# Attention in a two-layer encoder: product with v on token rows, softmax division behind it, four transposes back to channels

## The chip, the core and the metric

The kernel runs on one core of a Trainium2 chip. The metric is the device time in microseconds (us) of one execution. Three runs of the kernel before gave 1927.76, 1929.54 and 1931.59 us, with a median of 1929.54 us. One further execution was profiled; its own time was 1926.47 us, of which 1924.7 us are the span of the profile. The TensorE clock has two levels here, 2.4 and 1.2 GHz; the profile shows the granted clock as 1.00 and 0.50.

## What is computed

Two layers over 512 tokens and 1024 channels; each is a half-step SwiGLU, a mixer, and a second half-step SwiGLU. The mixer has windowed attention with 8 heads on 2 key heads, beside a state-space branch; both are normalized and go through one output projection. Cut to what matters:

```python
s = jnp.where(mask, q @ k * 0.125 + bias, NEG_INF)      # 128 queries, up to 384 keys
m = jnp.maximum(jnp.max(s, axis=-1, keepdims=True), sink)
p = jnp.exp(s - m)
denom = jnp.sum(p, axis=-1, keepdims=True) + jnp.exp(sink - m)
o = jnp.einsum('bnkgqs,bnskd->bnqkgd', p / denom, v)     # a: (512, 512)
x = x + concat(rms_norm(a, attn_out_norm), rms_norm(ssm, ssm_out_norm)) @ w_out
```

All of it is float32. Large products are made of three single-pass products of rounded parts (`mm3`, lines 216 to 218); attention's product with v and the transposes are plain float32.

## The kernel before

All activations lie with channels on the 128 partitions and 512 tokens along the row. Weights stream from memory in blocks of up to 128x2048; ScalarE rounds each block to its high part (line 199) and VectorE, in some places GpSimd, makes the low part (line 202), in two halves. There are two buffers for the high parts and two for the low parts, so a block's rounding waits until the products with the block two before it are done.

The mixer's work is a list of named steps, `ORDER` (line 43): a program walks through it and emits each step. The framework then places the instructions of each engine by an estimate of its own, so that steps of the list interleave; the order that came out is fixed in the program. Each engine runs its own list strictly in order.

The steps that matter here run per block n of 128 tokens and key head kv, so there are eight units per layer; a block has 2, 3, 3 and 2 key blocks kb:

- `as` (`a_scores`, line 951): for each of 4 heads two products into one PSUM bank (965, 966); VectorE adds the bias and finds the maximum (968); ScalarE makes the exponentials and their sums (975).
- `an` (`a_norm`, line 979): VectorE forms the denominators (985, 986) and divides the exponentials, one instruction per head (990).
- `ao` (`a_out`, line 992): for each key block, TensorE transposes the four heads' probabilities (998); the copy out of PSUM is VectorE's for odd key blocks (1001) and ScalarE's for even ones (1003).
- `pv` (`a_pv`, line 1008): the product with v (1013). v is the stationary operand, 64 columns of it per key head, the turned probabilities of four heads are the moving one, 512 wide; the two key heads use the two halves of the array. The result has channels on partitions. VectorE multiplies by the norm's gain (1022), ScalarE rounds to the high part (1024) and squares (1025), VectorE makes the low part (1027), GpSimd (VectorE for the last block) adds squares up into `acc_a` (1029, 1030).
- `ws` (`norm_ws`): the output projection's state-space half, products of 12 matmuls for each of eight output blocks, each followed by a multiplication and an addition to x (1066, 1068).
- After the list come the `wa` products, the output projection's attention half. They need all four blocks of the attention output, the high parts first and the low parts soon after. The sum of squares is turned into a factor by `rstd_a`, which begins with four matmuls against a column of ones (325), and `rstd_b` (341, 344).
- `ffn` follows; its first products need the high and low parts of the new x. VectorE makes the low parts (283), one 128x512 block at a time. In layer 0 VectorE also has the many small preparations of layer 1's state-space tables to do.

Of the kernel before, what the change touches and what calls it, by code (L numbers as in the profile page):

```python
# [9 lines left out]
F32R = mybir.dt.float32r  # L10
I32 = mybir.dt.int32
AF = mybir.ActivationFunctionType
# [4 lines left out]
P = 128  # L17
T = 512
# [24 lines left out]
l0 ui0 pu2 pu3 ui2 ui1 si0 k l1 ui3 v vt q0 si1 sc0 sc1 l2 q1 si2 l3 L0 q2 si3 q3 sc2 L1 so0 L2 as0 sc3 L3 an0  # L43
so2 as1 so1 so3 yt0 ao0 yt1 an1 as2 an2 ao1 glu as3 ao2 sn pv0 as4 ws0 an3 ao3 ws1 as5 an4 ws2 ao4 ws3 an5 as6
an6 pv1 ws4 ws5 ao5 as7 ws6 an7 ao7 ao6 pv2 ws7 pv3
# [30 lines left out]
class Emit:  # L76
# [242 lines left out]
    def rstd_a(self, acc, n, w=T):  # L319

        V = self.V
        b = self.bank()
        c = w // P
        for j in range(c):
            self.T.matmul(b[:, j:j + 1], acc[:, j * P:(j + 1) * P], self.ones, start=True, stop=True)  # L325
        s = self.slot()
        m, y, t = s[:, 0:c], s[:, 4:4 + c], s[:, 8:8 + c]
        V.tensor_scalar(m, b[:, 0:c], 1.0 / n, EPS, op0=ALU.mult, op1=ALU.add)
        self.bfree(b)
# [425 lines left out]
    def mixer(self, l, st, after):  # L755
# [223 lines left out]
        def a_norm(n, kv):  # L979
            k0, k1 = at[n]["k"]  # L980
            nk = (k1 - k0) * P
            sm = at[n]["sm"]
            c4 = slice(kv * 4, kv * 4 + 4)
            den, t = sm[:, 16:24], sm[:, 24:32]
            V.tensor_tensor(out=den[:, c4], in0=den[:, c4], in1=t[:, c4], op=A)
            V.reciprocal(den[:, c4], den[:, c4])
            for i in range(4):
                hd = kv * 4 + i
                p = at[n]["p"][kv][:, i * T:i * T + nk]
# [18 lines left out]
        def a_pv(n):  # L1008
            k0, k1 = at[n]["k"]
            o = self.bank()  # L1010
            for kb in range(k0, k1):
                for kv in range(2):
                    TE.matmul(o[kv * 64:kv * 64 + 64], vt[:, kb * P + kv * 64:kb * P + kv * 64 + 64], at[n][kv][kb - k0],
                              start=kb == k0, stop=kb == k1 - 1, tile_position=(0, kv * 64))
            for kv in range(2):
                self.free(*at[n][kv])

            if not abuf:
                abuf.extend([self.slot(4, True), self.slot(4, True)])
            cs = slice(n * T, (n + 1) * T)  # L1020
            f, q = self.slot(), self.slot()
            V.tensor_tensor(out=f.rearrange("p (i t) -> p i t", i=4), in0=o.rearrange("p (i t) -> p i t", i=4),
                            in1=ga.rearrange("p (i o) -> p i o", o=1).to_broadcast([P, 4, P]), op=M)
            S.copy(abuf[0][:, cs].bitcast(F32R), f)
            S.activation(q, o, AF.Square)
            self.bfree(o)
            V.tensor_tensor(out=abuf[1][:, cs].bitcast(F32R), in0=f, in1=abuf[0][:, cs], op=B)
            eng = V if n == 3 else Gp
            eng.tensor_tensor(out=q[:, 0:256], in0=q[:, 0:256], in1=q[:, 256:512], op=A)
            eng.tensor_tensor(out=acc_a[:, n * P:(n + 1) * P], in0=q[:, 0:P], in1=q[:, P:2 * P], op=A)  # L1030
            self.free(f, q, at[n]["sm"])
# [91 lines left out]
        def norm_ws(d):  # L1123
            if d == 0:
# [6 lines left out]
                 "as": lambda i: a_scores(*units[i]), "an": lambda i: a_norm(*units[i]),  # L1131
                 "ao": lambda i: a_out(*units[i]), "pv": a_pv, "yt": y_turn, "glu": lambda _: glu(),
# [13 lines left out]
        dg = self.rstd_a(acc_a, 512)  # L1146
# [125 lines left out]
def _cols(v):  # L1272
    return v.reshape(-1, P).T
# [11 lines left out]
def lay(inp):  # L1285
# [3 lines left out]
    g = []  # L1289
# [70 lines left out]
```

## Time and profile before

| | |
|---|---|
| median of three runs | 1929.54 us (1927.76 to 1931.59) |
| profiled execution, its own time | 1926.47 us |
| its span | 1924.7 us |
| TensorE busy | 1865.4 us, 97% |
| VectorE busy | 1123.4 us, 58% |
| ScalarE busy | 626.5 us, 33% |
| GpSimd busy | 714.8 us, 37% |

The stretches that the change touches are about 485 to 608 us (layer 0: attention, then `wa`, then the start of the second SwiGLU) and 1430 to 1560 us (layer 1). In the rows, PE is TensorE's matmul stream, PEld its loading of stationary operands, DVE VectorE, ACT ScalarE, POOL GpSimd. A float32 matmul appears as two matmul records (two passes), a transpose as one. The duration of one matmul runs until its result has drained, and successive ones overlap; how fast a train of them goes is seen from the start times.

### The profile page before, as it was taken

The page shows a single profiled execution, that of the slowest core. Times are in us where ns is not written, and L with a number is a line of the kernel's source. Part 1 is how long each engine was busy: PE and PEld are TensorE (multiplying, and loading weights), DVE is VectorE, ACT ScalarE, POOL GpSimd, SP SyncE. Part 2 cuts the span into 40 slices and gives each one's busy share as a digit, 9 for nine tenths or more (in the row PEclk, how much of TensorE's full clock was granted, in tenths as well). Part 3 has the DMA queues.
Part 4 walks back from the last instruction along what each step waited for, and adds up shares of the span by engine and source line. Part 5 has one row for each costly group of instructions (what it writes and reads, how often), then busy time and mean ns, then how long its engine had stood idle before and what let it go on. Part 6 is the DMA issues. An engine that isn't in the chain of part 4 may idle for free. (4 is left out here: it accounts for less than half of the span.)

```text
span 1924.7 us, 23787 instructions
## 1 busy us (share of the span) xinstructions
PE 1865.4 (97%) x9416; PEld 1510.5 (78%) x9416; DVE 1123.4 (58%) x1713; ACT 626.5 (33%) x954; POOL 714.8 (37%) x596
## 2 busy tenths in 40 slices
PE   8999999997998999999999999999989999999997
PEld 6888888886767888888878888888766678888886
DVE  8646545569888635355674453436697673434435
ACT  5223223322733323223332222224236342222223
POOL 2049899237233015093483351103452230201102
PEclk9999999998899999999999999999989999999998
DMA  5533434576011223233333234424640122222321
GB/s 202 165 121 123 160 125 156 160 244 229 31 67 61 98 104 121 99 131 115 108 134 114 99 133 129 137 98 142 232 171 23 65 79 98 88 107 82 107 97 46
DMA packets 86232, 231.12 MB, mean 120 GB/s; under 512 B 31160, under 2 KB 38504, under 8 KB 70376
## 3 DMA queue, kind: packets, MB, share of 16 engines
q1 hardware_dynamic: 84888, 228.51, 35.0%
q8 instruction: 74, 1.21, 0.3%
q10 hardware_dynamic: 1232, 1.09, 0.2%
q14 instruction: 38, 0.31, 0.0%
HBM read 201.11 MB, written 34.75 MB: 123 GB/s over the span
## 5 line engine op out<-in xcount | busy, mean ns | idle before, releaser
L216 PE MATMUL psum<-blk,whi 128*128 128x512 f32 (+1 forms) x2446 | 954.4, 393 | 9.7 <-ACT blk L277 6.4
L217 PE MATMUL psum<-blk,whi 128*128 128x512 f32 (+1 forms) x2446 | 953.7, 390 | 8.2 <-DVE blk L283 8.2
L218 PE MATMUL psum<-blk,wlo 128*128 128x512 f32 (+1 forms) x2446 | 952.0, 390 | 1.4 <-DVE wlo L202 0.9
L216 PEld LDWEIGHTS psum<-blk,whi 128*128 128x128 f32 x2446 | 462.0, 189 | 108.6 <-ACT blk L277 6.9
L217 PEld LDWEIGHTS psum<-blk,whi 128*128 128x128 f32 x2446 | 461.2, 189 | 106.3 <-DVE blk L283 12.9
L218 PEld LDWEIGHTS psum<-blk,wlo 128*128 128x128 f32 x2446 | 461.2, 189 | 97.9 <-DVE wlo L202 2.0
L199 ACT CAST whi<-raw 128x1024 fp32r<-128x1024 f32 (+1 forms) x310 | 303.4, 1027 | 683.3 <-PE psum L217 476.1
L202 DVE TENSOR_TENSOR wlo<-raw,whi 128x1024 fp32r<-128x1024 f32 (+1 forms) x288 | 419.2, 1490 | 40.6 <-ACT whi L199 30.7
L381 DVE TENSOR_TENSOR blk<-psum,blk 128x512 f32<-128x512 f32 x88 | 60.6, 691 | 343.7 <-PE psum L218 340.2
L407 POOL TENSOR_TENSOR xtile<-xtile,blk 128x512 f32<-128x512 f32 x64 | 88.1, 1378 | 374.3 <-DVE blk L405 370.1
L405 DVE SCALAR_TENSOR_TENSOR blk<-psum,blk 128x512 f32<-128x512 f32 x94 | 64.9, 690 | 214.9 <-PE psum L218 208.9
L380 ACT ACTIVATE blk<-blk 128x512 f32<-128x512 f32 x88 | 55.4, 632 | 301.9 <-DVE blk L378 297.4
L694 POOL TENSOR_TENSOR blk<-blk,blk 128x512 f32<-128x512 f32 x64 | 86.8, 1367 | 92.5 <-PE psum L707 51.7
L378 DVE TENSOR_TENSOR blk<-psum,blk 128x512 f32<-128x512 f32 x88 | 60.2, 688 | 85.7 <-PE psum L218 85.2
L295 POOL TENSOR_TENSOR blk<-blk,blk 128x512 f32<-128x512 f32 x30 | 45.6, 1518 | 155.1 <-ACT blk L288 154.3
L202 POOL TENSOR_TENSOR wlo<-raw,whi 128x1024 fp32r<-128x1024 f32 x22 | 60.4, 2752 | 110.2 <-ACT whi L199 110.0
L695 POOL TENSOR_TENSOR blk<-blk,blk 128x512 f32<-128x512 f32 x64 | 88.1, 1378 | 29.3 <-PE psum L707 14.4
L697 POOL TENSOR_TENSOR blk<-blk,blk 128x512 f32<-128x512 f32 x49 | 77.7, 1590 | 2.4
L385 DVE TENSOR_TENSOR blk<-blk,blk 128x512 fp32r<-128x512 f32 x88 | 76.4, 870 | 0.7 <-ACT blk L384 0.7
L283 DVE SCALAR_TENSOR_TENSOR blk<-xtile,consts,blk 128x512 fp32r<-128x512 f32 x48 | 58.7, 1239 | 10.6 <-ACT blk L277 10.6
L1068 POOL TENSOR_TENSOR xtile<-xtile,blk 128x512 f32<-128x512 f32 x24 | 33.7, 1425 | 72.8 <-DVE blk L1066 68.1
L295 POOL TENSOR_TENSOR blk<-blk 128x512 f32<-128x512 f32 x12 | 19.1, 1595 | 99.4 <-ACT blk L288 99.2
(227 smaller groups left out, 1343.0 us busy)
## 6 DMA issues: line engine op xcount, KB each, us to landing
raw<-w SPq DMA_DIRECT2D x123, 1024.0 KB, 4.8
raw<-w SPq DMA_DIRECT2D x32, 896.0 KB, 4.5
fd<-blk SPq DMA_DIRECT2D x32, 256.0 KB, 2.7
ed<-blk SPq DMA_DIRECT2D x32, 256.0 KB, 3.4
blk<-ed SPq DMA_DIRECT2D x32, 256.0 KB, 5.9
blk<-fd SPq DMA_DIRECT2D x32, 256.0 KB, 4.3
tb<-blk SPq DMA_DIRECT2D x12, 512.0 KB, 2.9
blk<-tb SPq DMA_DIRECT2D x24, 256.0 KB, 6.3
```

Source lines behind the costliest of these rows:

```text
L199: self.S.copy(hi[:, c], raw[:, c])
L202: eng.tensor_tensor(out=lo[:, c], in0=raw[:, c], in1=hi[:, c].bitcast(F32), op=ALU.subtract)
L216: t.matmul(out, wh, xh, start=start, stop=False)
L217: t.matmul(out, wh, xl, start=False, stop=False)
L218: t.matmul(out, wl, xh, start=False, stop=stop)
L295: eng.tensor_tensor(out=acc, in0=acc, in1=sq, op=ALU.add)
L385: V.tensor_tensor(out=lo.bitcast(F32R), in0=s, in1=hi, op=ALU.subtract)
L405: V.scalar_tensor_tensor(t, ps, 0.5, R, op0=ALU.mult, op1=ALU.mult)
L407: (V if last else self.G).tensor_tensor(out=self.x[d], in0=self.x[d], in1=t, op=ALU.add)
L694: Gp.tensor_tensor(out=full(o), in0=mat(a), in1=pwo(w, 0), op=M)
L695: Gp.tensor_tensor(out=full(t), in0=mat(b), in1=pwo(w, 1), op=M)
L697: Gp.tensor_tensor(out=o, in0=o, in1=t, op=sg)
```

## The change

The product with v is turned round. The turned probabilities of one head and key block (128 keys by 128 queries) become the stationary operand and 64 columns of v the moving one, so that the result has tokens on partitions and the eight heads' 64 channels side by side. The division by the denominator is no longer applied to the exponentials; it is applied once per block to that result, in one VectorE instruction that reads PSUM (line 1013 of the new file). ScalarE squares the result with a running sum per token (1016), which gives the sum of squares without the ones-matmuls and without GpSimd. Four transposes per block (1026) then bring channels back to partitions; gain, high part and low part follow as before (1029, 1032, 1033). All copies of turned probabilities are ScalarE's (991). The channels of the attention output now stand in their natural order, and the weights and gains are laid out to match. In `ORDER` the `an` steps are gone, `pt` steps are new, and `ws7` stands behind `pv3` instead of before it.

```diff
-so2 as1 so1 so3 yt0 ao0 yt1 an1 as2 an2 ao1 glu as3 ao2 sn pv0 as4 ws0 an3 ao3 ws1 as5 an4 ws2 ao4 ws3 an5 as6
-an6 pv1 ws4 ws5 ao5 as7 ws6 an7 ao7 ao6 pv2 ws7 pv3
+so2 as1 so1 so3 yt0 ao0 yt1 as2 ao1 glu as3 ao2 sn pv0 as4 ws0 pt0 ao3 ws1 as5 ws2 ao4 ws3 as6
+pv1 ws4 pt1 ws5 ao5 as7 ws6 ao7 ao6 pv2 pv3 pt2 ws7 pt3
...
-        def a_norm(n, kv):
...
-                V.tensor_scalar(p, p, den[:, hd:hd + 1], None, op0=M)
...
-                if kb % 2:
-                    V.tensor_copy(pt, b)
-                else:
-                    S.copy(pt, b)
+                S.copy(pt, b)
...
-            for kb in range(k0, k1):
-                for kv in range(2):
-                    TE.matmul(o[kv * 64:kv * 64 + 64], vt[:, kb * P + kv * 64:kb * P + kv * 64 + 64], at[n][kv][kb - k0],
-                              start=kb == k0, stop=kb == k1 - 1, tile_position=(0, kv * 64))
+            for kv in range(2):
+                for i in range(4):
+                    c = (kv * 4 + i) * 64
+                    for kb in range(k0, k1):
+                        TE.matmul(o[:, c:c + 64], at[n][kv][kb - k0][:, i * P:(i + 1) * P],
+                                  vt[:, kb * P + kv * 64:kb * P + kv * 64 + 64], start=kb == k0, stop=kb == k1 - 1)
...
+            V.tensor_tensor(out=den, in0=den, in1=t, op=A)
+            V.reciprocal(den, den)
+            f, q = self.slot(), self.slot()
+            V.tensor_tensor(out=f.rearrange("p (h e) -> p h e", h=8), in0=o.rearrange("p (h e) -> p h e", h=8),
+                            in1=den.rearrange("p (h o) -> p h o", o=1).to_broadcast([P, 8, 64]), op=M)
+            self.bfree(o)
+            S.activation(q, f, AF.Square, accum_out=acc_a[:, n:n + 1])
...
+        def a_turn(n):
...
+            for j in range(4):
+                TE.transpose(b[:, j * P:(j + 1) * P], f[:, j * P:(j + 1) * P], self.ident)
...
+            V.tensor_tensor(out=g.rearrange("p (i t) -> p i t", i=4), in0=b.rearrange("p (i t) -> p i t", i=4),
                             in1=ga.rearrange("p (i o) -> p i o", o=1).to_broadcast([P, 4, P]), op=M)
+            S.copy(abuf[0][:, cs].bitcast(F32R), g)
+            V.tensor_tensor(out=abuf[1][:, cs].bitcast(F32R), in0=g, in1=abuf[0][:, cs], op=B)
...
-        dg = self.rstd_a(acc_a, 512)
+        dg = self.rstd_c(acc_a, 512, 4)
```

How the instructions stand in a row, at the places of which the prediction speaks. First TensorE in layer 0, at block 0's product with v. Before (`L1013` is the product, `L998` a transpose; blk_423, blk_2989 and blk_2991 are buffers that hold turned probabilities, blk_2989 also v):

```order
L966 MATMUL psum<-blk_2988,blk_3428 128x384
L1013 MATMUL psum<-blk_2989 64x512
L1013 MATMUL psum<-blk_423,blk_2989 64x512 x2
L998 MATMUL psum<-consts,blk_3745 128x128 x8
L1013 MATMUL psum<-blk_2991,blk_2989 64x512
```

And now (`L1004` is the product, `L989` a transpose):

```order
L989 MATMUL psum<-consts,blk_3733 128x128 x4
L1004 MATMUL psum<-blk_2989 128x64
L1004 MATMUL psum<-blk_2989,blk_423 128x64
L989 MATMUL psum<-consts,blk_3733 128x128 x8
L1004 MATMUL psum<-blk_2989 128x64
L1004 MATMUL psum<-blk_2989,blk_423 128x64 x2
```

Four products of 512 columns have become sixteen of 64 columns for this block; they still interleave with the transposes of the blocks behind.

Second, TensorE at the end of attention in layer 0, where the `wa` products begin (`L216` reading whi_4121 and blk_3917, the high parts). Before:

```order
L1013 MATMUL psum<-blk_2991,blk_2989 64x512
L998 MATMUL psum<-consts,blk_4172 128x128 x8
L1013 MATMUL psum<-blk_423,blk_2989 64x512
L1013 MATMUL psum<-blk_2989 64x512
L1013 MATMUL psum<-blk_3161,blk_2989 64x512
L325 MATMUL psum<-consts,blk_2989 128x1 x2
L1013 MATMUL psum<-blk_423,blk_2989 64x512
L325 MATMUL psum<-consts,blk_2989 128x1
L216 MATMUL psum<-blk_3917,whi_4121 128x512 x4
L216 MATMUL psum<-blk_3917,whi_4270 128x512 x2
L217 MATMUL psum<-blk_3918,whi_4121 128x512
```

And now (whi_3941 is the block of `ws7`, `L1026` are the transposes back; blk_3963 holds the high parts, blk_3964 the low ones):

```order
L1004 MATMUL psum<-blk_2989,blk_423 128x64
L1026 MATMUL psum<-consts,blk_423 128x128 x4
L217 MATMUL psum<-blk_3823,whi_3941 128x512
...
L218 MATMUL psum<-blk_3836,wlo_3942 128x512
L1026 MATMUL psum<-consts,blk_423 128x128 x4
L216 MATMUL psum<-blk_3963,whi_4112 128x512 x4
L216 MATMUL psum<-blk_3963,whi_4301 128x512 x3
L217 MATMUL psum<-blk_3964,whi_4112 128x512
```

The last products of `ws7` stand between the product with v of the last block and its transposes, and nothing stands between those transposes and the `wa` products.

Third, VectorE at the same place. Before (`L1022` and `L1027` are gain and low part of the last block, `L1068` the addition to x behind `ws7`, `L202` half of a weight block's low part):

```order
L202 TENSOR_TENSOR wlo_4271<-raw_3956,whi_4270 128x1024
L1068 TENSOR_TENSOR xtile<-xtile,blk_4257 128x512
...
L1022 TENSOR_TENSOR blk_3161<-psum,consts 128x512
L471 TENSOR_SCALAR blk_4546<-blk_4546 128x32
L473 SCALAR_TENSOR_TENSOR blk_4546<-blk_4546 128x32 x3
L1027 TENSOR_TENSOR blk_3918<-blk_3161,blk_3917 128x512
```

And now (`L1069` and `L1071` are the multiplication and addition behind `ws7`, `L1029` and `L1033` gain and low part):

```order
L1069 TENSOR_TENSOR blk_3939<-psum,blk_3939 128x512
L338 SCALAR_TENSOR_TENSOR blk_2989<-blk_2989 128x4
L1029 TENSOR_TENSOR blk_4297<-psum,consts 128x512
L1071 TENSOR_TENSOR xtile<-xtile,blk_3939 128x512
L336 SCALAR_TENSOR_TENSOR blk_2989<-blk_2989 128x4
L202 TENSOR_TENSOR wlo_4302<-raw_3947,whi_4301 128x1024
L468 TENSOR_SCALAR blk_4573<-blk_4573 128x32
L571 TENSOR_TENSOR blk_4573<-blk_4573 128x32
L572 TENSOR_TENSOR blk_4573<-blk_4573 128x32
L337 TENSOR_TENSOR blk_2989<-blk_2989 128x4
L1033 TENSOR_TENSOR blk_3964<-blk_4297,blk_3963 128x512
```

The addition to x and the low part of a weight block have moved from ahead of the last block's gain to between its gain and its low part.

## Rows read from the trace of the kernel before

**Rows 1.** The page: busy time, share of the span, instructions of each engine.

```profile
PE 1865.4 (97%) x9416; PEld 1510.5 (78%) x9416; DVE 1123.4 (58%) x1713; ACT 626.5 (33%) x954; POOL 714.8 (37%) x596
```

**Rows 2.** Busy time by engine in four stretches (length; PE, PEld, DVE, ACT, POOL; clock, DMA).

```profile
485.00:570.00 85.00, 82.80 (x425) 56.65 (x422) 68.97 (x181) 53.12 (x128) 23.87 (x18) 0.96 0.14 51
570.00:608.00 38.00, 32.31 (x136) 25.49 (x137) 37.49 (x139) 15.20 (x23) 17.74 (x14) 0.96 0.08 28
1430.00:1519.00 89.00, 84.35 (x457) 57.07 (x455) 72.76 (x181) 55.59 (x132) 26.18 (x20) 1.00 0.14 51
1519.00:1560.00 41.00, 37.98 (x158) 30.04 (x159) 28.82 (x37) 14.64 (x23) 19.34 (x12) 0.96 0.12 39
```

**Rows 3.** TensorE's waits in layer 0, 485 to 608 (total us, times, longest).

```profile
PE psum L217 <- DVE blk L283: 5.1, 2, 4.0
PE psum L216 <- DVE blk L968: 1.1, 1, 1.1
```

**Rows 4.** The same in layer 1, 1430 to 1560.

```profile
PE psum L217 <- DVE blk L283: 2.2, 2, 1.4
PE psum L879 <- DVE blk L856: 1.5, 1, 1.5
```

**Rows 5.** The product with v alone (L1013): its PE and PEld time by stretch.

```profile
485.00:570.00 85.00, 13.58 (x40) 3.06 (x40) 0.96 0.14 51
1430.00:1519.00 89.00, 12.88 (x40) 3.11 (x40) 1.00 0.14 51
```

**Rows 6.** TensorE in order of time (start, duration): trains of small matmuls.

```profile
527.84 0.95 PE L325 MATMUL psum<-consts,blk 128*128 128x1 f32 x8
528.65 1.07 PE L998 MATMUL psum<-consts,blk 128*128 128x128 f32 x8
529.48 0.48 PE L216 MATMUL psum<-blk,whi 128*128 128x512 f32 x1
...
545.54 0.38 PE L966 MATMUL psum<-blk,blk 64*128 64x256 f32 x1
545.85 0.39 PE L965 MATMUL psum<-blk,blk 128*128 128x256 f32 x1
546.17 0.38 PE L966 MATMUL psum<-blk,blk 64*128 64x256 f32 x1
```

**Rows 7.** Groups by line (busy us, mean ns; idle before, and its releaser).

```profile
L990 DVE TENSOR_SCALAR blk<-blk,blk 128x256 f32<-128x256 f32 (+1 forms) x64 | 24.8, 449 | 0.4
L1001 DVE COPY blk<-psum 128x512 f32<-128x512 f32 x20 | 13.5, 683 | 1.6 <-PE psum L998 1.6
L1003 ACT COPY blk<-psum 128x512 f32<-128x512 f32 x20 | 11.9, 595 | 25.5 <-PE psum L998 25.5
L1022 DVE TENSOR_TENSOR blk<-psum,consts 128x512 f32<-128x512 f32 x8 | 5.5, 683 | 1.5 <-PE psum L1013 1.5
```

**Rows 8.** All engines in order of time at attention's end, layer 0.

```profile
559.79 1.99 ACT L199 CAST whi<-raw 128x1024 fp32r<-128x1024 f32 x2 [3.12 <-PE psum L217]
...
561.23 1.22 DVE L202 TENSOR_TENSOR wlo<-raw,whi 128x1024 fp32r<-128x1024 f32 x1
...
562.36 2.85 DVE L1068 TENSOR_TENSOR xtile<-xtile,blk 128x512 f32<-128x512 f32 x1
...
569.87 0.38 PE L325 MATMUL psum<-consts,blk 128*128 128x1 f32 x2 [0.87 <-POOL blk L1030]
569.97 0.62 ACT L1024 CAST blk<-blk 128x512 fp32r<-128x512 f32 x1 [1.89 <-DVE blk L1022]
...
570.64 1.66 PE L216 MATMUL psum<-blk,whi 128*128 128x512 f32 x6 [0.39 <-ACT blk L1024]
```

**Rows 9.** Two stretches at half clock (columns as in Rows 2).

```profile
519.00:522.50 3.50, 3.26 (x8) 2.59 (x9) 3.50 (x12) 2.44 (x5) 1.28 (x1) 0.51 0.70 279
604.40:607.80 3.40, 3.22 (x8) 2.08 (x7) 3.40 (x11) 1.24 (x2) 0.52 (x1) 0.50 0.00 0
```

More of the change, by code (lines that the diff above doesn't have):

```diff
@@ L325, in rstd_a, with rstd_c @@
             self.T.matmul(b[:, j:j + 1], acc[:, j * P:(j + 1) * P], self.ones, start=True, stop=True)
+        s = self.rstd_c(b, n, c)
+        self.bfree(b)
+        return s
+    def rstd_c(self, b, n, c):
+        V = self.V
         s = self.slot()
@@ L977, in a_scores @@
             at[n]["p"][kv] = pp
-        def a_norm(n, kv):
[L980 to L989, printed above, removed]
-                V.tensor_scalar(p, p, den[:, hd:hd + 1], None, op0=M)
         def a_out(n, kv):
@@ L1015, in a_pv @@
             for kv in range(2):
                 self.free(*at[n][kv])
+            sm = at[n]["sm"]
+            den, t = sm[:, 16:24], sm[:, 24:32]
+            V.tensor_tensor(out=den, in0=den, in1=t, op=A)
[3 more added lines that the diff above has]
+                            in1=den.rearrange("p (h o) -> p h o", o=1).to_broadcast([P, 8, 64]), op=M)
@@ L1018, in a_pv @@
+            self.bfree(o)
+            S.activation(q, f, AF.Square, accum_out=acc_a[:, n:n + 1])
+            self.free(q, sm)
+            at[n] = f
+        def a_turn(n):
+            f = at.pop(n)
             if not abuf:
                 abuf.extend([self.slot(4, True), self.slot(4, True)])
+            b = self.bank()
+            for j in range(4):
+                TE.transpose(b[:, j * P:(j + 1) * P], f[:, j * P:(j + 1) * P], self.ident)
             cs = slice(n * T, (n + 1) * T)
-            f, q = self.slot(), self.slot()
@@ L1022, in a_pv @@
-            V.tensor_tensor(out=f.rearrange("p (i t) -> p i t", i=4), in0=o.rearrange("p (i t) -> p i t", i=4),
+            g = self.slot()
+            V.tensor_tensor(out=g.rearrange("p (i t) -> p i t", i=4), in0=b.rearrange("p (i t) -> p i t", i=4),
                             in1=ga.rearrange("p (i o) -> p i o", o=1).to_broadcast([P, 4, P]), op=M)
[L1024 to L1031, printed above, removed]
+            self.bfree(b)
+            S.copy(abuf[0][:, cs].bitcast(F32R), g)
+            V.tensor_tensor(out=abuf[1][:, cs].bitcast(F32R), in0=g, in1=abuf[0][:, cs], op=B)
+            self.free(f, g)
         z = [None] * 4
@@ L1260, in _lay_weights @@
         elif kind == "wa":
-            blk = _tiles(inp["w_out"][l][ATT_ORDER], ar(a[1] * P, a[1] * P + 512))
+            blk = _tiles(inp["w_out"][l][0:512], ar(a[1] * P, a[1] * P + 512))
         elif kind == "ws":
@@ L1290, in lay @@
     for l in range(L):
-        g += [_cols(inp["ffn1_norm"][l]), _cols(inp["mix_norm"][l]), _cols(inp["attn_out_norm"][l][ATT_ORDER]),
+        g += [_cols(inp["ffn1_norm"][l]), _cols(inp["mix_norm"][l]), _cols(inp["attn_out_norm"][l]),
               _cols(inp["ssm_out_norm"][l][SSM_ORDER]), _cols(inp["ffn2_norm"][l]), _cols(inp["ssm_b_glu"][l][SSM_ORDER])]
```

7 lines of the change are left out of this document (2 added, 5 removed).

## The prediction

> **What bounds the kernel now.** I read the page's first part, then the busy time by stretch where the change works, then what TensorE waits for there. TensorE is busy 97% of the span and VectorE 58% [rows 1]: outside the mixers a VectorE saving is worth nothing. In attention itself, TensorE is busy 82.8 of 85 us in layer 0 and 84.4 of 89 in layer 1; between attention and the second SwiGLU 32.3 of 38 and 38.0 of 41 [rows 2]. So TensorE's gaps in the four stretches are 2.2, 5.7, 4.7 and 3.0 us. Of these 1.5 us are a wait for the state-space branch [rows 4], which the change doesn't reach. What a lighter VectorE can give back is therefore at most 14.1 us, plus what the clock loses behind such gaps: two stretches of 3.4 us run at half clock [rows 9], and a third lies in layer 1 (the 0.96 of its last row [rows 2]). VectorE is at its limit only from 570 to 608 us, 37.5 of 38 [rows 2], where TensorE waits 5.1 us for the low parts of x, line 283 [rows 3]; in layer 1, without the table work, the same wait is 2.2 us [rows 4]. A microsecond that TensorE gets to do more in attention is thus nearly a microsecond of the kernel.
>
> **TensorE's own work.** The product with v takes 13.58 and 12.88 us, 26.5 in all, in 80 records [rows 5]: 20 matmuls per layer, two passes each. It is turned into 8 heads x 10 key blocks = 80 matmuls per layer, 320 passes in all, each with its own 128x128 stationary load and only 64 columns to stream. No row shows that form. The nearest is the ones-matmul, line 325: the same stationary shape, float32, two passes, 1 column; eight of them take 0.81 us, from 527.84 to 528.65, 0.101 each [rows 6]. The transposes have the same stationary shape and stream 128 columns in one pass, eight in 0.83 us, 0.104 each [rows 6]. With 1 and with 128 columns it takes the same, so the load sets the pace and 64 columns, streamed in about 0.05 us by the transposes' rate, hide beside it. The first of a train starts early, so for long trains I take 0.11 us. That gives 320 x 0.11 = 35.2 us. The new transposes are 4 per block, 32 x 0.104 = 3.3 us; the ones-matmuls of this norm fall away, 4 x 2 passes x 2 layers x 0.10 = 1.6 us. Sum: 35.2 + 3.3 - 1.6 - 26.5 = **+10.4 us**, all on the path. The lower bound is 0.101 per pass, +7.5. For the upper one the load isn't hidden: 0.10 + 0.05 = 0.155, +24.8. Farther still are the scores' products: 0.31 us apart for 256 columns [rows 6], although a 512-column product of rounded parts starts every 0.23 us (six in 1.66 us, the last one's drain included) [rows 8]; there about 0.2 us of load is exposed, which would be 0.25 per pass and +55. Those products change the number of rows from 128 to 64 and back at each step (128*128, 64*128 in the rows), which the new ones don't; I give that end no weight.
>
> A rule of the Trainium skill speaks against the change here. "TensorE: Matmul & The Clock Gate", Part 3, says that a stationary load overlaps with matmuls in flight only when it goes to other row groups. All new products use all row groups, so by it the upper bound would hold. The transposes, 128 rows each, contradict it: load and 128 columns together in 0.104 us. By rule the sum would be +24.8, by row +10.4; I follow the row and keep the rule as a rival.
>
> **VectorE, ScalarE, GpSimd.** VectorE loses the divisions, 24.8 us, and its share of the copies, 13.5; it gains eight multiplications like line 1022's, 5.5 us [rows 7]; with the small denominators merged it is some 35 us lighter over both layers. ScalarE gains 20 copies of 0.595 us, 11.9 us [rows 7], on 53 and 56 busy us in the two attention stretches [rows 2]: it has room on average, not everywhere, since exponentials and copies now queue on one engine and the product with v waits for the copies. No row prices that; nothing at best, 3 us a layer at worst (five copies in a row), and I take 1 a layer, **+2**. Below nothing it can't be, since ScalarE gets no instruction fewer on that way. GpSimd's additions were off the path but for the last ones' 0.87 us [rows 8], counted below.
>
> **The seam to the output projection** is where the order tells most. Count from the end of `ws7`'s last product. The four transposes take 0.4 us. VectorE first does `ws7`'s multiplication (0.68, the shape of line 1022), then the gain, 0.68 [rows 7]: about 1.7 with the small ones. ScalarE has the rounding of the second `wa` block ahead of the high part. That rounding waits for `ws7`'s products, whose buffer it takes (before it waited for the same, 3.12 us, but ten microseconds ahead of the seam), and lasts 1.99; the high part follows with 0.62 [rows 8]. So `wa` starts at about 2.8 and TensorE idles 2.4. Seven products of 0.23 carry it to 4.4. The low part stands on VectorE behind the addition to x, the weight block's low half, 1.22 [rows 8], and five small ones, 0.1 each. The addition took 2.85 when GpSimd worked beside it [rows 8] and can't be under the 0.68 of its shape; I take 1.4. Low part done: 1.7 + 1.4 + 1.2 + 0.5 + 0.7 = 5.5, a second idle of 1.1. Together 3.5 us (2.8 to 5) where before TensorE idled 0.87 + 0.39 = 1.26 [rows 8]: +2.3 a layer, **+4.6** (3 to 7.5). One more stretch of 3.4 us at half clock behind so long a gap costs what it does in [rows 9], half its length: **+1.7** (0 to 3.4).
>
> **What comes back.** The wait for the scores' bias step, line 968, 1.1 us [rows 3] in each layer, and the half clock behind it at 519 us [rows 9], 1.7: 3.9 at most; I take 3, as VectorE had been busy for 10 us with divisions and copies ahead of it. At the start of the second SwiGLU in layer 0 the 5.1 us should shrink to layer 1's 2.2, with the half clock at 604 us [rows 9]: 2.9 + 1.7; I take 4.5. Sum **-7.5**.
>
> **Sum**: 10.4 + 2 + 4.6 + 1.7 - 7.5 = +11.2 us on the profiled execution's 1926.47, which is 1937.7. That execution lies 3.1 us under the median of the runs, 1929.54; on the median the forecast is 1929.5 + 11.2 = **1941 us**.
>
> **Rivals.**
> 1. Faster: VectorE was the true pace of these stretches. For: 37.5 of 38 us busy at the end of layer 0, 69 of 85 before [rows 2]. Then all 14.1 us of gaps and three half-clock stretches, 5.1, come back, the seam hides behind quick VectorE work but for some 3 us, and the passes run at their lower bound: 7.5 + 3 - 19.2 = -8.7, 1921 us. It decides once the gaps that go outweigh 10 us of TensorE work. Against: in attention TensorE has only 2.2 us of gaps in layer 0. Chance 0.11.
> 2. About even: TensorE's work as forecast, but the gaps go almost entirely (-14) and the seam costs its lower bound: 10.4 + 3 + 2 - 14 = +1.4, 1931 us. Chance 0.15.
> 3. The loads aren't hidden: 24.8 in place of 10.4, 1955 us. Against: the transposes' row. Chance 0.11.
> 4. The clock: the last two blocks' products with v, 16 + 24 matmuls or 80 passes a layer, stand almost alone on TensorE. If they stream too little and fall to 1.2 GHz, they cost 80 x 0.11 more a layer, +17.6 or 1958 us. Against: the ones-matmuls and transposes of [rows 6] ran at full pace, in a mixed stretch, however. Chance 0.06.
>
> **How the numbers follow.** The forecast has 0.57, with its own range of 1934 to 1950 from the bounds of seam, copies and returns. Below it lie rivals 1 and 2, above it 3 and 4. The range that should hold 8 in 10 leaves out most of rival 1 and the far ends of 3 and 4: 1927 to 1956. About 0.2%, 3.9 us, is what a measurement of this kernel can tell from no change: faster than 1925.7 has 0.12 (rival 1 and a little of 2), within 1925.7 to 1933.4 has 0.16, slower 0.72.
>
> **What the profile after would show.** The passes of line 1004 start 0.10 to 0.11 us apart; 0.15 or more means rival 3, and 0.2 at a granted clock of 0.5 rival 4. TensorE's busy time in attention grows by some 5 us a layer. Behind the last transposes back there are two gaps before and in the `wa` products, the first released by line 1032, the second by 1033. The wait for line 283 in layer 0 comes down to about 2 us, and that for line 968 nearly vanishes. VectorE's busy time falls by some 35 us, ScalarE's rises by 12. I am wrong if the wait for 283 and the half clocks return more than the seam and the turned product take, or if ScalarE's copies make TensorE wait several microseconds a layer.

## The result, and the profile after

The changed kernel takes 1942.42 us in the median of four runs (1938.06 to 1945.59), the kernel before beside it 1928.65 (1925.71 to 1931.59): a ratio of 1.0068, with a 95% interval of 1.0046 to 1.0090. It is slower by 13.8 us, where 11.2 were forecast (1941 beside 1929.5), with the sign that was forecast. The same kernel run again later, against other runs of before, gave 1.0079 (1.0063 to 1.0095).

The profiled execution of the changed kernel took 1938.06 us, 11.6 more than that of before (1926.47), and is the fastest of its runs. The page's first lines, to be laid beside [rows 1]:

```profile
span 1936.3 us, 24217 instructions
## 1 busy us (share of the span) xinstructions
PE 1872.7 (97%) x9672; PEld 1540.5 (80%) x9672; DVE 1091.3 (56%) x1617; ACT 637.6 (33%) x982; POOL 711.2 (37%) x584
```

Where the time went can be read by setting the same matmul of TensorE side by side in the two traces, the n-th of line 216, whose order outside the mixers is the same. At 437 us, ahead of layer 0's attention, the changed kernel is 0.1 us early, and at 455 us 1.6 us early, since a stretch of 3.4 us at half clock at 444 us in the kernel before has no counterpart in it. Behind layer 0's mixer it is 4.4 us late, and behind layer 1's 11.9; between and behind the mixers this stays the same to 0.1 us, up to the last 20 us, which give back 0.3. So the two mixers cost 6.0 and 7.6 us. In the later run's trace they cost 6.1 and 7.5.

VectorE is 32 us lighter, ScalarE 11 us heavier, TensorE busy for 7 us more. The weight loads grew by 30 us: that is the turned product. Its own time in the two attention stretches, in the columns of [rows 5]:

```profile
484.00:572.00 88.00, 19.81 (x160) 19.10 (x160) 1.00 0.08 25
1430.00:1526.50 96.50, 19.80 (x160) 19.02 (x160) 0.98 0.13 48
```

39.6 us against 26.5, both with the drains of each train in them; counted from the start of each pass to the start of TensorE's next instruction, 34.8 against 25.4. TensorE's waits from attention to the start of the second SwiGLU, in layer 0 (total us, times, longest):

```profile
PE psum L217 <- DVE blk L283: 3.6, 3, 1.8
PE psum L217 <- DVE blk L1033: 2.2, 1, 2.2
PE psum L216 <- ACT blk L1032: 1.9, 1, 1.9
PE psum L969 <- ACT blk L1047: 1.7, 1, 1.7
PE psum L969 <- DVE blk L972: 0.8, 1, 0.8
...
```

The same in layer 1:

```profile
PE psum L217 <- DVE blk L283: 3.6, 2, 2.7
...
PE psum L216 <- ACT blk L1032: 1.9, 1, 1.9
...
PE psum L217 <- DVE blk L1033: 1.4, 1, 1.4
PE psum L969 <- ACT blk L1047: 0.9, 1, 0.9
```

Lines 1032 and 1033 are the rounding to the high part and the low part of the normalised attention (1024 and 1027 before), 972 is the scores' bias step (968 before), 1047 the state-space branch's activation (1044 before). Beside [rows 3, 4] the wait for 283 is down by 1.5 us in layer 0 and up by 1.4 in layer 1 (its longest there, 2.7 us, is the same in the later run; why it grew isn't shown). The waits at the seam, 1032 and 1033, hold 7.4 us in both layers; before, the two waits there held 0.87 + 0.39 = 1.26 in layer 0 [rows 8] and 1.1 in layer 1. Here is the seam of layer 0 in order of time (start, duration, engine; idle before in brackets), from `ws7`'s end at 571.8:

```profile
571.82 0.60 PE L1026 MATMUL psum<-consts,blk 128*128 128x128 f32 x4
572.02 0.69 DVE L1069 TENSOR_TENSOR blk<-psum,blk 128x512 f32<-128x512 f32 x1 [0.23 <-PE psum L218]
...
572.70 0.68 DVE L1029 TENSOR_TENSOR blk<-psum,consts 128x512 f32<-128x512 f32 x1
573.30 0.68 DVE L1071 TENSOR_TENSOR xtile<-xtile,blk 128x512 f32<-128x512 f32 x1
573.69 0.61 ACT L1032 CAST blk<-blk 128x512 fp32r<-128x512 f32 x1
...
573.92 2.39 POOL L202 TENSOR_TENSOR wlo<-raw,whi 128x1024 fp32r<-128x1024 f32 x1 [14.02 <-ACT whi L199]
573.97 3.42 DVE L202 TENSOR_TENSOR wlo<-raw,whi 128x1024 fp32r<-128x1024 f32 x1
...
577.67 0.68 DVE L1033 TENSOR_TENSOR blk<-blk,blk 128x512 fp32r<-128x512 f32 x1
```

The transposes back end at 572.4; two multiplications on VectorE (`ws7`'s, then the gain) and ScalarE's rounding of a weight block (1.99 from 571.79, not shown) stand ahead of the high part at 573.69, and 3.42 us of a weight block's low part ahead of 1033. This low part began 0.05 us behind GpSimd's of the other half and ended 1.1 us after GpSimd was done.

### The profile page after: what moved, and what is told of

It reads as the page before. It is cut to its first block, busy times and chain, and to the rows that moved or that the text cites. A ratio compares the mean times of both kernels' runs of the same rounds, so it can differ in the third digit from the quotient of the medians.

```text
span 1936.3 us, 24217 instructions
## 1 busy us (share of the span) xinstructions
PE 1872.7 (97%) x9672; PEld 1540.5 (80%) x9672; DVE 1091.3 (56%) x1617; ACT 637.6 (33%) x982; POOL 711.2 (37%) x584
## 4 chain that ended last, share of the span: by engine, by line
PE 82%; DVE 9%; POOL 3%; issue 2%; DMA 1%; ACT 1%; SPq 0%; DVEq 0%; ACTq 0%; POOLq 0%
PE psum L217 25%; PE psum L216 25%; PE psum L218 25%; PE psum L1004 2%; DVE wlo L202 2%; DVE blk L853 1%; DVE blk L283 1%; POOL blk L698 1%; PE psum L970 1%; POOL blk L701 1%; PE psum L989 1%; PE psum L969 1%; PE psum L729 1%; POOL blk L699 1%; DVE blk L935 1%
## 5 line engine op out<-in xcount | busy, mean ns | idle before, releaser
L216 PE MATMUL psum<-blk,whi 128*128 128x512 f32 (+1 forms) x2446 | 953.3, 392 | 10.1 <-ACT blk L277 6.2
L216 PEld LDWEIGHTS psum<-blk,whi 128*128 128x128 f32 x2446 | 461.0, 189 | 106.7 <-ACT blk L277 6.6
L199 ACT CAST whi<-raw 128x1024 fp32r<-128x1024 f32 (+1 forms) x310 | 303.4, 1027 | 653.0 <-PE psum L217 442.4
L202 DVE TENSOR_TENSOR wlo<-raw,whi 128x1024 fp32r<-128x1024 f32 (+1 forms) x288 | 420.7, 1495 | 27.4 <-ACT whi L199 17.6
L202 POOL TENSOR_TENSOR wlo<-raw,whi 128x1024 fp32r<-128x1024 f32 x22 | 60.0, 2735 | 115.6 <-ACT whi L199 95.1
L1071 POOL TENSOR_TENSOR xtile<-xtile,blk 128x512 f32<-128x512 f32 x24 | 36.8, 1550 | 71.4 <-DVE blk L1069 69.5
L283 DVE SCALAR_TENSOR_TENSOR blk<-xtile,consts,blk 128x512 fp32r<-128x512 f32 x48 | 54.7, 1154 | 10.9 <-ACT blk L277 10.9
```

The lines of the kernel that those rows point to most:

```text
L199: self.S.copy(hi[:, c], raw[:, c])
L202: eng.tensor_tensor(out=lo[:, c], in0=raw[:, c], in1=hi[:, c].bitcast(F32), op=ALU.subtract)
L216: t.matmul(out, wh, xh, start=start, stop=False)
L283: self.V.scalar_tensor_tensor(lo.bitcast(F32R), self.x[d], self.gains[:, st["g"] + d:st["g"] + d + 1], hi, op0=ALU.mult, op1=ALU.subtract)
```

## The experiments

The kernels ran in three groups, each beside its own runs of before (medians 1930.60, 1929.21 and 1930.61). For reading them one conversion helps. A mean granted clock of 1 is 2.4 GHz throughout; a stretch at 1.2 GHz does about half the work in its time (from pass to pass 213 ns in place of 112, below), so on a TensorE that is busy 97% of the span a mean clock of c loses at most about (1 - c) x span. "Lost" in this table is that number for the profiled run. It is an estimate, and too high: of the 60.8 us at half clock in the trace of before TensorE was busy for 43.3, and the last 10 to 13 us of every kernel here stand at half clock with TensorE busy for only 0.7 to 1.4. From run to run, by a straight line through spans and clocks, a thousandth of the clock goes with 0.8 us in the 45 runs of before and with 1.4 in the ten of the changed kernel, not with 1.9. So the last column shows large differences only; one of a few us in it says nothing.

| kernel | ratio to before (95%) | profiled span | clock | lost | span without it |
|---|---|---|---|---|---|
| before | 1 | 1924.7 | 0.984 | 31 | 1894 |
| changed | 1.0068 (1.0046 to 1.0090) | 1936.3 | 0.987 | 25 | 1911 |
| changed, again | 1.0079 (1.0063 to 1.0095) | 1939.1 | 0.987 | 25 | 1914 |
| changed, product with v twice | 1.0289 (1.0274 to 1.0304) | 1993.9 | 0.975 | 50 | 1944 |
| changed, 128 columns a pass | 1.0109 (1.0087 to 1.0131) | 1943.8 | 0.982 | 35 | 1909 |
| changed, last block not turned back | 1.0047 (1.0032 to 1.0062) | 1932.7 | 0.985 | 29 | 1904 |
| changed, ws6 kept back | 1.0085 (1.0071 to 1.0098) | 1944.5 | 0.983 | 33 | 1911 |
| changed, ws7 early | 1.0122 (1.0109 to 1.0135) | 1951.3 | 0.978 | 43 | 1908 |
| changed, odd copies on VectorE | 1.0085 (1.0072 to 1.0098) | 1944.8 | 0.983 | 33 | 1912 |
| before, no division | 1.0045 (1.0029 to 1.0060) | 1943.6 | 0.977 | 45 | 1899 |
| before, all copies on ScalarE | 1.0022 (1.0011 to 1.0032) | 1930.6 | 0.987 | 25 | 1905 |
| before, both of these | 1.0040 (1.0026 to 1.0054) | 1933.5 | 0.983 | 33 | 1901 |
| before, product in pairs | 0.9985 (0.9977 to 0.9994) | 1925.9 | 0.984 | 31 | 1895 |

### The price of a pass

```diff
-                    for kb in range(k0, k1):
+                    for kb in list(range(k0, k1)) * 2:
                         TE.matmul(o[:, c:c + 64], at[n][kv][kb - k0][:, i * P:(i + 1) * P],
```

> The changed kernel with every product with v issued twice into the same sum, 320 passes more in the program (the output is then twice what it should be before normalisation; only the time is read). My theory: a pass costs TensorE about 0.11 us and nothing hides it, so 320 x 0.109 = +35 us on the changed kernel, 1942 + 35 = 1977 us. Rival A, the turned product partly fills gaps that TensorE has anyway: +20 to +28 us, 1962 to 1970 us. Rival B, the load of each pass is exposed as soon as trains are long: 0.155 a pass, +50 us, 1992 us.

Measured: 1987.62 us (1985.52 to 1995.70), 45 us over the changed kernel's 1942.4, or 43 by the difference of the two ratios. That is more than my theory's 35 and less than rival B's 50; what is over goes with the clock, which neither had (0.975 to 0.981 in its four runs, the profiled one the slowest of them). The doubled product by stretch (PE, PEld; clock):

```profile
500.00:546.00 46.00, 10.28 (x84) 9.96 (x85) 0.96 0.07 24
546.00:567.00 21.00, 16.63 (x78) 16.25 (x77) 0.51 0.14 51
567.00:600.00 33.00, 18.42 (x160) 18.26 (x160) 1.00 0.01 3
1430.00:1532.00 102.00, 10.19 (x82) 9.77 (x82) 0.93 0.28 97
1532.00:1553.00 21.00, 17.16 (x79) 16.75 (x78) 0.51 0.09 36
1553.00:1585.00 32.00, 18.42 (x160) 18.26 (x160) 1.00 0.00 1
```

The 84 passes in the first stretch, nearly all at full clock, took 10.28 us, 0.12 each with drains; the 78 in the second 16.63, or 0.21. From pass to pass the median is 112 ns at full clock (465 passes) and 213 at half (148). In both layers a train of the first two blocks' products, 64 and 76 passes in a row, falls into some 21 us at half clock. The last two blocks' products, of which rival 4 speaks, are the 160 passes of the third stretch in each layer; 140 and 122 of them stand in one row, from 581.1 and from 1567.3, and they ran at full clock, 0.115 each with drains. All engines in the first stretch at half clock and in the longest row, in the columns of [rows 2]:

```profile
546.00:567.00 21.00, 21.00 (x90) 19.80 (x90) 2.03 (x9) 5.20 (x20) 0.00 (x0) 0.51 0.14 51
581.00:597.00 16.00, 16.00 (x146) 16.00 (x145) 0.80 (x2) 1.80 (x4) 0.00 (x0) 1.00 0.01 2
```

The time from 546 to 567 us in the changed kernel:

```profile
546.00:567.00 21.00, 21.00 (x153) 18.86 (x153) 7.86 (x24) 10.47 (x32) 2.55 (x2) 1.00 0.00 1
```

TensorE is busy for all of the time in the three rows. In the changed kernel 89 of the 153 matmuls are products with v, in rows of at most 30 passes with full products and transposes between. How long such products stand alone can't be the whole reason, for the row of 140 passes ran at full clock too; why the clock fell at 546 and 1532 us isn't shown. So the price of a pass is 0.11 us, and 0.21 where it is at half clock, and rival 4's mechanism, that these products bring the clock down by standing alone, didn't show where rival 4 expected it. By the last column of the table the doubled kernel is 33 us longer than the changed one, for 320 passes 0.10 each.

### Whether the load or the columns pace it

```diff
-                    c = (kv * 4 + i) * 64
+                    c = min((kv * 4 + i) * 64, 384)
...
-                        TE.matmul(o[:, c:c + 64], at[n][kv][kb - k0][:, i * P:(i + 1) * P],
-                                  vt[:, kb * P + kv * 64:kb * P + kv * 64 + 64], start=kb == k0, stop=kb == k1 - 1)
+                        TE.matmul(o[:, c:c + 128], at[n][kv][kb - k0][:, i * P:(i + 1) * P],
+                                  vt[:, kb * P:kb * P + 128], start=kb == k0, stop=kb == k1 - 1)
```

> The changed kernel with 128 columns of v in place of 64 in each product, the sums of the heads then overlapping (the output is wrong; only the time is read). My theory: the pass is paced by its load, so a pass still starts 0.112 us after the last one and the time stays within 2 us of the changed kernel. Rival: the columns pace it; at the transposes' rate or slower a pass with 128 columns takes longer by 0.03 to 0.05 us, 320 of them +10 to +16 us.

Measured: a pass with 128 columns starts 112 ns after the last one in the median, as with 64. Its time alone, two rows like those of the changed kernel above:

```profile
484.00:575.00 91.00, 20.55 (x160) 19.10 (x160) 1.00 0.09 30
1430.00:1535.00 105.00, 21.19 (x160) 19.17 (x160) 0.90 0.14 48
```

41.7 us in place of 39.6, drains included (in the mean 0.115 from pass to pass in place of 0.110). The load sets the pace, and twice the columns are nearly free. The kernel was at 1948.64 us, 4 us over the same group's run of the changed one; the profile has it at a clock of 0.982, where a run of the changed kernel has the same span, 1943.8 us. My 2 us were too narrow for the clock; the rival's 10 to 16 are out.

### The seam

Three runs. The first takes the wait for the last transposes away: `a_turn(3)` returns at once, and the third block writes the fourth's columns too.

```diff
             f = at.pop(n)
+            if n == 3:
+                self.free(f)
+                return
...
-            S.copy(abuf[0][:, cs].bitcast(F32R), g)
-            V.tensor_tensor(out=abuf[1][:, cs].bitcast(F32R), in0=g, in1=abuf[0][:, cs], op=B)
+            for cs in ([cs, slice(3 * T, 4 * T)] if n == 2 else [cs]):
+                S.copy(abuf[0][:, cs].bitcast(F32R), g)
+                V.tensor_tensor(out=abuf[1][:, cs].bitcast(F32R), in0=g, in1=abuf[0][:, cs], op=B)
```

> The changed kernel with the last block not transposed back: the third block's result is written in its place as well (the output is wrong in the last 128 tokens; only the time is read). ws7's products then stand between the transposes and the wa products, with nothing that the first wa product waits for behind them. My theory: the seam's two gaps go (7.4 us in both layers), with four transposes a layer (0.8 us) and the half clock behind the gap of layer 1 (3.4 us): -6 to -10 us beside the changed kernel, 1932 to 1936 us. Rival A: the gaps hang on VectorE's and GpSimd's other work and only change their releaser, -2 us or less.

Measured: 1938.64 us (1934.46 to 1940.64), 5.8 less than the changed kernel's 1944.43 in the same group, a little short of what was expected, and the transposes that fell away, 0.8 us, are in it. TensorE's waits in layer 0 from 560 to 650 us, all of them:

```profile
PE psum L217 <- DVE blk L283: 5.7, 4, 1.9
PE psum L218 <- DVE wlo L202: 0.4, 1, 0.4
```

Both gaps are gone; of the 7.4 us some 2 in layer 0 come back as a longer wait for 283 (3.6 to 5.7), and layer 1 gives 0.6 more (3.6 to 3.0). Rival A is out: the gaps were the seam's own.

The second keeps `ws6` back so that more products stand behind the last product with v:

```diff
-pv1 ws4 pt1 ws5 ao5 as7 ws6 ao7 ao6 pv2 pv3 pt2 ws7 pt3
+pv1 ws4 pt1 ws5 ao5 as7 ao7 ao6 pv2 pv3 pt2 ws6 pt3 ws7
```

> The changed kernel with one more block of the state-space output (ws6) kept back until behind the last product with v, so that twelve full products stand between the last transposes back and the first wa product on either side. My theory: the two gaps at the seam (7.4 us in both layers in the changed kernel's trace, 2.5 before) shrink to about what they were, -4 to -5 us beside the changed kernel, 1938 us, less up to 1 us a layer that ws6 covered earlier. Rival A: the gaps hang on VectorE and only move, within 1 us of 1942.4. Rival B: without ws6 in between the products with v stand longer alone and the clock falls, +4 us or more.

Measured: 1945.74 us (1941.21 to 1947.93), no gain. The trace shows why, and that it doesn't test what it should: the last division is done at 569.5, but its transposes still run at 572.54, behind all of `ws6` and `ws7`. The planner orders by its own estimate of when an input is ready, and the written order is only a preference.

```profile
568.84 0.69 DVE L1013 TENSOR_TENSOR blk<-psum,blk 128x512 f32<-128x512 f32 x1 [4.96 <-PE psum L1004]
...
572.54 0.60 PE L1026 MATMUL psum<-consts,blk 128*128 128x128 f32 x4
```

The third puts `ws7` back ahead of `pv3`:

```diff
-pv1 ws4 pt1 ws5 ao5 as7 ws6 ao7 ao6 pv2 pv3 pt2 ws7 pt3
+pv1 ws4 pt1 ws5 ao5 as7 ws6 ao7 ao6 pv2 ws7 pv3 pt2 pt3
```

> The changed kernel with ws7 ahead of the last block's product with v again, where it stood before the change, so that both last blocks are transposed back directly ahead of the wa products and nothing covers the last block's division. My theory: the first gap at the seam grows by the multiplication by the denominators, the transposes and half of the next multiplication, 1.5 to 2 us a layer, so +3 to +4 us beside the changed kernel, 1946 us. Rival: the seam is set by VectorE's other work and the place of ws7 doesn't matter, within 1 us of 1942.4.

Measured: 1951.90 us (1950.59 to 1954.76), 9.5 over the changed kernel; but not for the reason given. Its waits at the seam of layer 0:

```profile
PE psum L1026 <- DVE blk L1013: 2.5, 1, 2.5
PE psum L216 <- ACT blk L1032: 1.4, 1, 1.4
```

In layer 1 they are 0.3 and 1.4. That is 5.6 us where the changed kernel has 7.4. So what the division's wait costs, the low part's wait gives back, and in waits the place of `ws7` costs nothing. The 15 us between the two spans go with the clock, 0.978 against 0.987: at half clock TensorE is busy for 69.5 us in this trace and for 32.9 in the changed kernel's. Two of its stretches, of 6.8 us each at 578 and 623 us, stand behind the seam that the edit changed; whether the edit brings them isn't shown. Another stands at a place that the edit doesn't reach. From 484 to 514 us, with TensorE's instructions in the same order up to 565, this kernel:

```profile
484.00:514.00 30.00, 28.26 (x180) 22.12 (x180) 11.85 (x33) 23.04 (x56) 0.90 (x1) 0.83 0.00 1
```

And the changed one:

```profile
484.00:514.00 30.00, 28.23 (x209) 22.48 (x210) 16.36 (x41) 27.41 (x62) 3.20 (x3) 1.00 0.01 2
```

### How far the clock goes by itself

The changed kernel, unaltered.

> The changed kernel once more, unaltered. Its first profile had a granted clock of 0.987 and is the fastest of its runs; in the first experiments a stretch of 10 to 14 us at half clock stood at 493 us, also in the one where TensorE's instructions are the same up to 565 us (ws7 early). Theory A: that stretch comes and goes from run to run with one program, so the time of the changed kernel scatters by 5 to 7 us with its clock (0.982 to 0.987) and its profile may show the stretch. Theory B: it belongs to the edits; then this profile has none at 493 us and the clock is 0.985 or more.

Measured: six runs from 1939.81 to 1948.33 us, with clocks of 0.983 to 0.987; with the first four, ten runs of one program over 10 us, those at 0.986 and 0.987 under 1941, those at 0.982 and 0.983 over 1943. Its profile has only 3.4 us at half clock at 494.8, not the 10 to 14 of three edited kernels. So both theories hold by half: the clock makes one program scatter by several us from run to run, and the long stretch at 493 belongs to something in the edited ones (all four runs with `ws7` early have 0.975 to 0.979) that TensorE's rows ahead of it don't show. What that is stays open.

### What a lighter VectorE is worth

The kernel before without the division; with all copies on ScalarE; with both.

```diff
-            V.tensor_tensor(out=den[:, c4], in0=den[:, c4], in1=t[:, c4], op=A)
-            V.reciprocal(den[:, c4], den[:, c4])
-            for i in range(4):
-                hd = kv * 4 + i
-                p = at[n]["p"][kv][:, i * T:i * T + nk]
-                V.tensor_scalar(p, p, den[:, hd:hd + 1], None, op0=M)
+            return
...
-                if kb % 2:
-                    V.tensor_copy(pt, b)
-                else:
-                    S.copy(pt, b)
+                S.copy(pt, b)
```

> The kernel before with the division of the probabilities left out altogether (24.8 us of VectorE; the output lacks the softmax division, only the time is read). It shows what a lighter VectorE alone is worth. My theory: the wait for the scores' bias step and the half clock behind it, and some of the wait for the low parts of x in layer 0, 3 to 5 us, so 1924 to 1926 us beside 1928.7. Rival (VectorE is the pace of these stretches): 9 us or more, 1919 us or less. Rival (the gaps have other causes): within 1.5 us.

> The kernel before with the copies of all turned probabilities on ScalarE and nothing else changed: 13.5 us less on VectorE, 11.9 more on ScalarE. My theory: waits for ScalarE of about 1 us a layer against about as much back from VectorE's waits, so within 2 us of 1928.7. Rival A: ScalarE's queue of exponentials and copies holds up the product with v, +3 to +6 us. Rival B: VectorE's relief counts, -3 us or more.

> The kernel before without the division and with all copies on ScalarE: VectorE is then as light as in the changed kernel (38 us less), while TensorE's products are those of before (the output lacks the softmax division, only the time is read). My theory after the first runs: each half alone gave 4 and 9 us more, so together still no gain, 1930 to 1940 us; the lighter VectorE isn't what the changed kernel gets anything from. Rival A: VectorE was the pace and only both halves together free it, 1925 us or less. Rival B: the waits of the two add up, 1943 us.

Measured: 1939.78, 1934.69 and 1935.32 us, 9.2, 4.1 and 6.1 over before in the same groups. None is faster, with up to 41 us less on VectorE (1082.6 busy in the last, 1123.4 in [rows 1]). For the division my theory of 3 to 5 us back was wrong, and its rival of 9 more so. Its profiled run, the slowest of its six, is 19 us longer than before's, up to 14 of them lost clock (0.977). In the last one the wait that I had put down to the heavy VectorE stands as before, to the digit [rows 3] (4.5 and 4.2 us in the other two):

```profile
PE psum L217 <- DVE blk L283: 5.1, 2, 4.0
PE psum L216 <- ACT blk L1016: 2.4, 1, 2.4
...
PE psum L1005 <- ACT blk L995: 0.9, 1, 0.9
```

What stands ahead of 283 on VectorE, in this trace and in that of before, is the next layer's table work, with one multiplication in between. VectorE has 41 us less to do in all, but from 570 to 608 us it is still busy for 36.1 of 38 us, where it was 37.5 [rows 2]. The copies alone cost 4 us, and their trace has them at layer 0's seam, where TensorE waits 3.3 us for the high part and 2.7 for a weight block's low part. Whether ScalarE's longer queue does that or the order that the planner then makes isn't settled by these runs, since each edit moves the order too.

The copies the other way, odd blocks back on VectorE in the changed kernel:

```diff
-                S.copy(pt, b)
+                if kb % 2:
+                    V.tensor_copy(pt, b)
+                else:
+                    S.copy(pt, b)
```

> The changed kernel with the copies of odd key blocks on VectorE again, as before the change. My theory: ScalarE's copies cost about 1 us a layer because the product with v waits for them, so this gives back 2 us, 1940.4 us, and the wait of the state-space branch's transposed output for ScalarE (1.7 us in layer 0) goes. Rival A: the copies cost nothing, TensorE's time is set by its own work, 1942 within 1 us. Rival B: VectorE is needed for the new norm, and copies on it put the gaps back that the change removed, +2 to +4 us.

Measured: 1.0085 (1.0072 to 1.0098) against 1.0068 and 1.0079 for the changed kernel: nothing comes back, and without the lost time the two spans are alike (1912 and 1911). The wait for 1047, which I had ascribed to ScalarE's copies, is 1.7 and 1.5 us here, no less. Rival A's nothing and rival B's 2 to 4 us can't be told apart here.

### A faster version

The doubled product says that TensorE's own work is the time. In the kernel before it can be cut: there a pass of one key head starts 7 ns behind its partner of the other, if both have their probabilities, and 24 of 80 passes did. The order was changed so that the products find them ready:

```diff
-so2 as1 so1 so3 yt0 ao0 yt1 an1 as2 an2 ao1 glu as3 ao2 sn pv0 as4 ws0 an3 ao3 ws1 as5 an4 ws2 ao4 ws3 an5 as6
-an6 pv1 ws4 ws5 ao5 as7 ws6 an7 ao7 ao6 pv2 ws7 pv3
+so2 as1 so1 so3 yt0 ao0 yt1 an1 as2 an2 ao1 glu as3 ao2 sn as4 ws0 pv0 an3 ao3 ws1 as5 an4 ws2 ao4 ws3 an5 as6
+an6 pv1 ws4 ws5 ao5 as7 ws6 an7 ao7 ao6 ws7 pv2 pv3
```

> The kernel before with another order: pv0 behind as4 and ws0, pv2 behind ws7, so that the products with v find all turned probabilities ready and stand in one row. In the trace of before a pass that starts 7 ns behind its partner of the other key head costs nothing of its own, and one that stands alone 0.43 to 0.52 us; 40 passes in pairs would take 17 us of TensorE in place of 25.4. My theory: TensorE's own work is the time, so -4 to -7 us, 1924 to 1926 us. Rival A: the gain is given back at the seam or in waits for copies, within 1.5 us of 1930. Rival B: the clock falls in the longer trains, +3 us or more.

Measured: 1926.30 us (11 runs, 1924.34 to 1928.50), 2.9 less than before, ratio 0.9985 (0.9977 to 0.9994); it is the fastest of all. The product by stretch:

```profile
484.00:575.00 91.00, 10.53 (x40) 2.74 (x40) 0.96 0.14 48
1430.00:1530.00 100.00, 12.66 (x40) 3.10 (x40) 0.94 0.12 44
```

The start of a train of twelve passes in pairs, in order of time (start, duration):

```profile
554.16 0.64 PE L1013 MATMUL psum<-blk,blk 128*64 128x512 f32 x1
554.17 0.64 PE L1013 MATMUL psum<-blk 128*64 128x512 f32 x1
554.64 0.59 PE L1013 MATMUL psum<-blk,blk 128*64 128x512 f32 x1
554.65 0.59 PE L1013 MATMUL psum<-blk 128*64 128x512 f32 x1
```

Layer 0 went from 13.58 [rows 5] to 10.53, layer 1 only from 12.88 to 12.66: there the planner put the passes apart again. The passes that start right behind a partner went from 12 to 17 in layer 0 and from 12 to 13 in layer 1. That is 3.3 us less of TensorE, where 4 to 7 were expected, but it is not shown to be the 2.9 us of the kernel. The 11 runs had a clock of 0.984 to 0.987, the 17 of before 0.981 to 0.986. At 0.984 the median spans are 1926.4 us (3 runs) and 1926.9 (9 runs), at 0.986 1924.9 (4) and 1925.0 (3). So at equal clock 0.1 to 0.5 us is left, and the rest goes with the clock; whether the new order raises it isn't shown. The two profiled runs, both at 0.984, have spans of 1925.9 us with the new order and 1924.7 with the old.

## Why the prediction was right

**TensorE's own work: right.** Forecast +10.4. The passes are 0.110 us apart in the mean of 293 that follow another (0.11 taken), so the product costs 34.8 us (35.2 forecast), 9.4 more than before. With 32 transposes and without the ones-matmuls, both at their forecast prices, that is 11.1. The doubled product confirms the price on the whole kernel, and the 128-column pass confirms the reason, that the load sets the pace and the columns hide beside it. Here the rule weighed in the prediction falls: the Trainium skill, "TensorE: Matmul & The Clock Gate", Part 3, has a load overlap with matmuls in flight only if it goes to other row groups. No pass here changes its row group, and 128 columns take no longer from pass to pass than 64 in the median, 5 ns longer in the mean. Rival 3 is out.

**The seam: right in sum, by other rows.** Forecast +4.6 with two gaps of 2.4 and 1.1; measured 1.9 + 2.2 and 1.9 + 1.4, 7.4 in all, against the 1.26 a layer that the forecast took for before: +4.9. The high part came earlier than counted (573.69 is 1.9 behind `ws7`'s end), the low part later: VectorE's 1.22 for the low part of a weight block became 3.42 while GpSimd ran the same operation, where I had stretched the addition to x instead (1.4 taken, 0.68 measured). Taking the wait away, with 0.8 us of transposes, gave the kernel 5.8 us.

**The extra half clock: right.** 1.7 taken; layer 1's seam has a stretch of 6.8 us in place of 3.4, in both traces of the changed kernel; layer 0's has none.

**ScalarE's copies: not shown.** 2 us taken. In the trace the wait for the activation of the state-space branch went from 1.3 us in both layers to 2.6, but it is as long with odd copies on VectorE, and no run gave the copies' price apart from the order's. From the changed kernel to the one with copies back it is nothing that can be measured.

**What comes back: the step that failed.** I took -7.5: -3 for line 968 with its half clock, -4.5 for line 283 with its own. Both stretches at half clock, at 519 and 604 us [rows 9], are gone from both traces of the changed kernel, -3.4. The wait for 968 came down from 2.2 us in both layers to 0.8, -1.4. But the wait for 283 as a whole returned nothing: 5.1 + 2.2 before, 3.6 + 3.6 after. "Should shrink to layer 1's 2.2" took the heavy VectorE for its cause; the kernel before with 41 us less on VectorE has the same 5.1, and what stands ahead of 283 there is the next layer's table work. Why layer 1's wait grew stays open. So -4.9 in place of -7.5.

**The sum.** 11.1 + 4.9 + 1.7 + 1.3 - 4.9 = +14.1 from the parts, and the two mixers cost 6.0 + 7.6 = 13.6 us in the trace. The profiled runs differ by 11.6, because the changed one was 1.6 us ahead by the time attention began and got 0.3 back at its end, which no step foresaw; the later trace has a stretch at half clock at 444 us, as before has. That the forecast of 11.2 met 11.6 so closely is partly luck: the returns were put 2.6 too high, and a chance of the clock of 1.9 lay on the other side. On the medians, where the changed kernel ran at 0.982 to 0.987, it is 13.8, the first time and the second.

**The rivals.** 1 (VectorE the pace) and 2 (the gaps go almost entirely) are out: none of the three kernels with a lighter VectorE gained, though their order moved too, and the gaps at the seam grew. 3 is out by the time from pass to pass. 4 did not happen here, and in the doubled product the last two blocks' 160 passes a layer ran at full clock; the 157 passes at 0.21 there are of the first two blocks, and their cause is open.

## What to carry to other kernels

Where TensorE is busy nearly all of the time, count its passes first: a small product that needs a stationary load of its own for each 64 columns costs a load's time, here 0.11 us at full clock, and work taken off another engine returns only the waits that end on that engine last. Before a wait is credited to a lighter engine, look at what is queued directly ahead of the awaited instruction: here it was work of the next layer, and a VectorE that was lighter by 41 us still had it there. With a planner that orders by its own times, every edit also moves the order, and here the clock often moved too; compare several runs, at equal clock where there are enough, with the mean granted clock beside each time.

## What the runs showed of the hardware that was not expected

- A TensorE without a gap can stand at half clock: in the doubled product it was busy for 21.0 of 21 us, 78 of 90 matmuls products of 64 columns, at 0.51, in both layers. A row of 140 such passes later in the same run stood at 1.00, so the kind of product doesn't settle it; the cause is open.
- At half clock the pass takes 0.213 us, at full clock 0.112: the load that paces it slows with the clock.
- VectorE's low part of a weight block (128x1024) took at most 1.23 us in the changed kernel wherever GpSimd was idle (127 times). With GpSimd at work beside it, it took 2.13 us in the median (97 times), and 3.416 once, when it began just behind the same operation on GpSimd. Line 202 on VectorE in the changed kernel, both widths (min, median, max in ns):

```profile
L202 DVE TENSOR_TENSOR wlo<-raw,whi x288: 1079/1225/3416, 22.1 to 1903.3; 128x1024 fp32r<-128x1024 f32 x112, 128x896 fp32r<-128x896 f32 x32
```

- One program's clock differs from run to run (0.982 to 0.987 in ten runs), and its times with it, by 10 us in this kernel, as much as most of the edits here were worth.
